# Expert layers of a decoder trunk in written program order, with a new start and a half-fp32 output projection

## The chip, the cores and the metric

The kernel runs on one core of a Trainium2 chip. The metric is the time of one execution in microseconds (us): the median over the runs shown. Five engines work side by side, each on its own queue of instructions: TensorE (PE in the profile, PEld for its weight loads), VectorE (DVE), ScalarE (ACT), GpSimd (POOL) and SyncE (SP), which here only starts DMA transfers. An engine waits on semaphores for the others; the program is scheduled ahead of time, so what stands in an engine's queue, and in which order, is fixed when it is built.

## The reference

Two layers over 256 tokens of width 1024. Layer 0 mixes tokens by a short gated convolution, layer 1 by differential attention; each is followed by a PEER expert layer. Every sub-layer is modulated by shift, scale and gate vectors made from `c`, and ended by a layer norm. Cut to what matters here:

```python
def ada_mod(c, w, b):
    m = jax.nn.silu(c) @ w + b
    shift, scale, gate = jnp.split(m, 3, axis=-1)
    return shift[:, None, :], 1.0 + scale[:, None, :], 1.0 + gate[:, None, :]

def short_conv_mixer(h, w_in, conv_w, w_out):
    gb, gc, xv = jnp.split(h @ w_in, 3, axis=-1)
    z = gc * xv
    zc = conv_w[0] * zp[:, 0:S] + conv_w[1] * zp[:, 1:S + 1] + conv_w[2] * zp[:, 2:S + 2]
    return (gb * zc) @ w_out

def peer_ffn(h, w_q, sub_keys, u, v):          # 8 heads, 2 x 128 keys, 16384 experts
    q = (xc @ w_q).reshape(PEER_CHUNK, PEER_HEADS, 2, PEER_HALF)
    s = jnp.einsum('thpd,pnd->thpn', q, sub_keys)
    sv, si = lax.top_k(s, PEER_TOPK)            # top 16 of each half
    cand_s = sv[:, :, 0, :, None] + sv[:, :, 1, None, :]
    top_s, pos = lax.top_k(cand_s, PEER_TOPK)   # top 16 of the pairs
    g = jax.nn.softmax(top_s, axis=-1)
    act = jax.nn.gelu(jnp.einsum('td,thkd->thk', xc, u[idx]), approximate=False)
    return jnp.einsum('thk,thkd->td', g * act, v[idx])

# per layer: h = x*scale + shift; f = mixer(h) or peer_ffn(h)
#            x = layer_norm(ALPHA * x + gate * f, ln_g, ln_b)
```

## The kernel before

The expert layer doesn't gather: it computes all 128 x 128 experts densely and masks. Experts come in 128 blocks of 128. A **w_q step** (16 of them) projects the queries, and a **U step** (128) the pre-activations of one block; each is 24 matmuls of 256 columns, because every fp32 operand is split into a high and a low fp32r part and three products are summed (`mm3`, lines 141 to 143). After two U steps ScalarE runs a gelu (L805) into `ring`. A **V step** (128) is 12 matmuls of 512 columns into the four accumulators `acc` (L874). A **G step** (`G_step`, 32 for each of three chunks of 46, 42 and 40 blocks) turns the picked expert numbers into a mask: DVE builds two one-hot tiles A and B (L825 to L829), PE multiplies them (L838) and DVE multiplies the result into `ring` (L840).

Each weight tile of 512 KB is loaded by SP into a `raw` buffer and split: ACT copies the high part (L87), DVE subtracts to get the low part (L90; shown as `spt<-raw,spt`). `pipeline` starts the load and split of a step three steps ahead of its matmuls. The split tiles come from the pool `sp` of ten buffers, the raw ones from six (`STREAM`).

The picks are made beside this. `halves` takes the top 16 of each half of the keys (five DVE operations for each of 16 heads-and-halves and two token tiles), two such pieces after every w_q step from the fifth on. `topk(t)` then handles the pairs: sums in `cand`, eight heads of five operations, a softmax (an exp on ACT, L735, between DVE operations), twelve small operations on `f`, two rounds of one-hot look-ups (`eq` on DVE, `keys` copied by ACT, L766 to L774), and three PE transposes. A piece stands after every U step of the first chunk.

`fill` computes modulation vectors of later sub-layers: one column of `ada_w` is a 512 KB load and one DVE operation over 128 x 1024 (L177, `raw<-raw,csb`). In the expert layers it runs in the gaps of the third and last V chunk. `late` applies the norm's gain and bias to X (L297) for the residual, `prep` makes the gain and bias rows for the next norm.

Before the expert layers stands layer 0's convolution. `csb`, the silu of `c` on all partitions, is a 512 KB broadcast load; X comes as one load of 1 MB (L207 transposes it). `project_out` (L352) multiplies the convolution's output `y` by its weights, again in three products. Norm sums are L266 and L268; L286 writes the normalised X.

What sets the order: `ordered` pins DMA starts to program order while the convolution layer is built; after it, the scheduler that builds the program places every instruction by its own estimate of when it can run. Inside the expert layers all engines follow that scheduler, not the text.

Of the kernel before, what the change touches and what calls it, by code (L numbers as in the profile page):

```python
# [37 lines left out]
SPBUFS = 10  # L38
STREAM = 6
# [4 lines left out]
def tile_trunk(ctx: ExitStack, tc: tile.TileContext, x, c, columns, ada_w, ln_g, ln_b, conv_w_in_a, conv_w_in_b,  # L44
# [3 lines left out]
    dve, act, pool, pe = nc.vector, nc.scalar, nc.gpsimd, nc.tensor  # L48
# [99 lines left out]
    nc.sync.dma_start(csb, rows_bcast(c[0], D))  # L148
    X = const.tile([P, NT, D], F32, name="X")

# [14 lines left out]
    act.activation(csb, csb, AF.Silu)  # L165
# [7 lines left out]
    def ada_column(i, s, part, n, dst):  # L173

        w = raw()
# [3 lines left out]
    def ada_unit(i, s, part):  # L179
        a = small.tile([P, KC], F32, tag="ada", name="ada", bufs=2)  # L180
        for q in range(KC // 2):
            for f in [ada_column(i, s, part, n, a[:, n:n + 1]) for n in (2 * q, 2 * q + 1)]:
                f()
            yield
        at = slice(None), 2 * i + s, slice(KC * part, KC * part + KC)
        dve.tensor_tensor(mod[at], a, ada_bT[at], op=ALU.add)
        yield
# [30 lines left out]
    def ln_params(i, s):  # L218
        gb = raw(), raw()
# [15 lines left out]
    class Norm:  # L235
# [56 lines left out]
        def affine(self, _):  # L292

            gb = ln_params(self.i, self.s)
            for t in range(NT):
                for n, op in enumerate((ALU.mult, ALU.add)):
                    dve.tensor_tensor(X[:, t, :], X[:, t, :], gb[n], op=op)  # L297

# [39 lines left out]
    def project_out(w, yT, accs, engs):  # L338
        def first(q):
            return [load(w[(2 * q + kk) * P:(2 * q + kk + 1) * P, :], engs[kk]) for kk in range(2)]  # L340

        def second(q, parts):
            if q == 0:
                accs.extend(new_accs())
            yh, yl = yT[q]
            for t in range(NT):
                rows = slice(t * P, (t + 1) * P)
                for kk, (wh, wl) in enumerate(parts):
                    k = 2 * q + kk
                    for lhs, rhs, first, last in ((yh, wh, True, False), (yh, wl, False, False), (yl, wh, False, True)):  # L350
# [7 lines left out]
    def conv_mixer(j, hT, cp, fill, prep):  # L358
        gbT = [None] * KC
        gcT = [None] * KC  # L360
        yh = cp.tile([P, KC, T], F32R, name="yh")
        yl = cp.tile([P, KC, T], F32R, name="yl")

        def use(n, ps):
# [9 lines left out]
            y = cp.tile([P, T], F32, tag="y", name="y", bufs=2)  # L374
# [4 lines left out]
            dve.tensor_tensor(y, y, gbT[k], op=ALU.mult)  # L379
            copy(yh[:, k, :], y)  # L380
            last["y"] = sub(dve, yl[:, k, :], y, yh[:, k, :].bitcast(F32))
# [7 lines left out]
        def h_first(q):  # L389
# [3 lines left out]
            if q == 0:  # L393
# [623 lines left out]
```

## Time and profile before

| | before |
|---|---|
| median of 3 runs | 1957.79 us (1957.78 to 1961.25) |
| profiled execution | 1956.54 us |
| its span, first to last instruction | 1954.8 us |
| PE busy | 1885.1 us, 96% of the span |
| DVE busy | 1550.6 us, 79% |
| ACT busy | 905.3 us, 46% |
| mean granted TensorE clock | 0.988 |
| HBM read | 375.42 MB, 193 GB/s over the span |

The profile is of one execution, 1.25 us below the median. The span leaves 1.7 us outside of it. "Busy" is the union of an engine's instructions; the span minus PE's busy time, 69.7 us, is all that PE stood still. Matmuls overlap in the trace (a record of 283 ns begins every 120 ns or so), so PE's pace is read from counts in a stretch, not from the length of one record.

### The profile page before, as it was taken

To read this page: it belongs to the slowest core of one execution; us is meant where nothing else is said; L and a number is where in the kernel's file an instruction comes from. 1 tells how busy PE (TensorE), PEld (TensorE's weight loads), DVE (VectorE), ACT (ScalarE), POOL (GpSimd) and SP (SyncE) were. 2 spreads that over 40 slices of the span, in tenths; PEclk is the share of its full clock that TensorE was granted. 3 is DMA by queue.
4 is the path that set the end of the run, shared out by engine and by line. 5 is a ranking of instruction groups with operands and counts; after the bars stand their busy time and mean duration, and the time that the engine had idled before them with its cause. 6 is when DMAs were issued, how large, how long until landed. Compare 5 with 4: busy or idle time off the path is not lost.

```text
span 1954.8 us, 36946 instructions
## 1 busy us (share of the span) xinstructions
PE 1885.1 (96%) x14858; PEld 1720.6 (88%) x14858; DVE 1550.6 (79%) x3138; ACT 905.3 (46%) x1191; POOL 9.5 (0%) x28
## 2 busy tenths in 40 slices
PE   7969999999999999989899899999999999999897
PEld 6969999999999988867798799999999999888786
DVE  7989887887888888876677788878878766888755
ACT  4534555334444444434466545653444444444443
POOL 0000000000000000000100000000000000000000
PEclk9989999999999999999999999999999999999999
DMA  9955655556778765568753246555567555555563
GB/s 383 366 187 159 185 180 177 163 158 210 249 243 256 232 201 173 173 198 279 241 182 111 86 152 184 183 174 161 161 208 226 173 175 181 168 169 181 173 194 97
DMA packets 104412, 378.87 MB, mean 194 GB/s; under 512 B 11568, under 2 KB 12208, under 8 KB 104240
## 3 DMA queue, kind: packets, MB, share of 16 engines
q1 hardware_dynamic: 104096, 376.42, 59.8%
q8 instruction: 116, 1.90, 0.4%
q14 instruction: 56, 0.46, 0.1%
q10 hardware_dynamic: 144, 0.09, 0.0%
HBM read 375.42 MB, written 1.05 MB: 193 GB/s over the span
## 4 chain that ended last, share of the span: by engine, by line
PE 91%; DVE 5%; DMA 2%; issue 1%; ACT 1%; SPq 0%; DVEq 0%; ACTq 0%
PE acc L874 34%; PE ps L141 15%; PE ps L142 15%; PE ps L143 15%; PE ps L838 4%; DVE raw L177 2%; PE acc L352 2%; PE acc L142 2%; PE acc L141 2%; PE acc L143 2%; DVE spt L90 1%; DMA raw<-in_ada_w 1%; DMA X<-in_x 1%; PE ps L517 0%; DMA gsub<-in_attn_subln_g 0%
## 5 line engine op out<-in xcount | busy, mean ns | idle before, releaser
L87 ACT ACTIVATE spt<-raw 128x1024 fp32r<-128x1024 f32 x608 | 641.1, 1058 | 745.3 <-PE ps L142 416.5
L90 DVE TENSOR_TENSOR spt<-raw,spt 128x1024 fp32r<-128x1024 f32 x608 | 741.0, 1222 | 171.3 <-ACT spt L87 166.5
L141 PE MATMUL ps<-hh,spt 128*128 128x256 f32 x2400 | 684.9, 286 | 2.9 <-DVE hh L214 2.4
L142 PE MATMUL ps<-hl,spt 128*128 128x256 f32 x2400 | 681.0, 284 | 0.6 <-DVE hl L90 0.6
L143 PE MATMUL ps<-hh,spt 128*128 128x256 f32 x2400 | 680.5, 284 | 0.0
L874 PE MATMUL acc<-spt,wh 128*128 128x512 f32 x2048 | 565.9, 396 | 4.4 <-ACT wh L87 4.4
L141 PEld LDWEIGHTS ps<-hh,spt 128*128 128x128 f32 x2400 | 460.6, 192 | 6.8 <-issue 3.0
L142 PEld LDWEIGHTS ps<-hl,spt 128*128 128x128 f32 x2400 | 461.4, 192 | 4.0 <-DVE hl L90 0.9
L143 PEld LDWEIGHTS ps<-hh,spt 128*128 128x128 f32 x2400 | 461.3, 192 | 0.0
L874 PEld LDWEIGHTS acc<-spt,wh 128*128 128x128 f32 x2048 | 375.9, 188 | 75.8 <-ACT wh L87 4.6
L874 PE MATMUL acc<-spt,wl 128*128 128x512 f32 x1024 | 319.6, 392 | 3.6 <-DVE wl L90 3.6
L874 PEld LDWEIGHTS acc<-spt,wl 128*128 128x128 f32 x1024 | 191.9, 188 | 44.8 <-DVE wl L90 5.1
L177 DVE SCALAR_TENSOR_TENSOR raw<-raw,csb 128x1024 f32<-128x1024 f32 x96 | 116.1, 1223 | 57.8 <-DMA raw<-in_ada_w 57.7
L87 ACT ACTIVATE wh<-ring 128x512 fp32r<-128x512 f32 x128 | 79.9, 627 | 159.0 <-PE acc L874 148.9
L840 DVE SCALAR_TENSOR_TENSOR ring<-ps,ring 128x368 f32<-128x368 f32 (+2 forms) x192 | 98.1, 512 | 68.6 <-PE ps L838 68.0
L825 DVE TENSOR_TENSOR A<-iota_e,jT 128x1024 f16<-128x1024 f16 x192 | 131.0, 683 | 0.0
L829 DVE TENSOR_TENSOR B<-B,gT 128x368 f16<-128x368 f16 (+2 forms) x384 | 125.1, 334 | 4.0
L90 DVE TENSOR_TENSOR wl<-ring,wh 128x512 fp32r<-128x512 f32 x128 | 88.0, 689 | 38.7 <-ACT wh L87 38.2
L838 PEld LDWEIGHTS <-A 128*128 128x128 f16 x3072 | 91.0, 96 | 31.1 <-issue 14.3
L838 PE MATMUL ps<-B,A 128*128 128x46 f16 (+2 forms) x3072 | 111.7, 182 | 6.6 <-DVE B L829 6.6
L805 ACT ACTIVATE ring<-ps 128x512 f32<-128x512 f32 x128 | 74.7, 584 | 33.8 <-PE ps L143 33.7
L827 DVE TENSOR_TENSOR B<-iota_e,iT 128x368 f16<-128x368 f16 (+2 forms) x192 | 63.4, 331 | 0.0
(204 smaller groups left out, 1179.9 us busy)
## 6 DMA issues: line engine op xcount, KB each, us to landing
raw<-in_peer_u SPq DMA_DIRECT2D x256, 512.0 KB, 3.8
raw<-in_peer_v SPq DMA_DIRECT2D x256, 512.0 KB, 3.9
raw<-in_ada_w SPq DMA_DIRECT2D x96, 512.0 KB, 4.7
raw<-in_peer_w_q SPq DMA_DIRECT2D x32, 512.0 KB, 4.1
raw<-in_attn_w_qk SPq DMA_DIRECT2D x16, 512.0 KB, 4.4
raw<-in_conv_w_in_a SPq DMA_DIRECT2D x12, 512.0 KB, 10.2
raw<-in_conv_w_in_b SPq DMA_DIRECT2D x12, 512.0 KB, 10.2
raw<-in_conv_w_out SPq DMA_DIRECT2D x8, 512.0 KB, 7.2
```

The lines of the kernel that those rows point to most:

```text
L87: act.activation(o, i, AF.Copy, scale=scale)
L90: return eng.tensor_tensor(o, a, b, op=ALU.subtract)
L141: pe.matmul(ps, ah, bh, start=first, stop=False)
L142: pe.matmul(ps, ah, bl, start=False, stop=False)
L143: pe.matmul(ps, al, bh, start=False, stop=last)
L177: return lambda: dve.scalar_tensor_tensor(w, w, 1.0, csb, op0=ALU.mult, op1=ALU.mult, accum_out=dst)
L805: act.activation(ring[:, s:s + 2, :].rearrange("p j t -> p (j t)"), st["ps"], AF.Gelu)
L825: dve.tensor_tensor(by_two(A), numbers(0, KEYS), pairs(jT, KEYS), op=ALU.is_equal)
L829: dve.tensor_tensor(by_two(B[:, h]), by_two(B[:, 1]), pairs(gT[:, h], n), op=ALU.mult)
L838: pe.matmul(ps[:, t, :], A[:, t, :], B[:, h, t, :], start=h == 0, stop=h == 1)
L840: dve.scalar_tensor_tensor(r, ps.rearrange("p t j -> p j t"), 1.0 / GSCALE, r, op0=ALU.mult, op1=ALU.mult)
L874: pe.matmul(acc[t][hf], lhs[:, jj, rows], rhs[:, hf * 512:(hf + 1) * 512], start=first and jp == 0 and jj == 0, stop=last and last_pair an ...
```

## The change

Four edits. First, in both expert layers every instruction of PE, DVE and ACT, and every load of SP, is kept in program order from the end of the w_q loop on (`pinned`, and the wrapper `InOrder`); the `yield None` that flushed the pipeline there is gone. Second, the room for this: `cand`, `f`, `eq` and `keys` of `topk` get fixed places in the ring's spare part instead of `sp` buffers, `SPBUFS` goes from 10 to 9 and `STREAM` from 6 to 5, and two `side` buffers carry the columns of `fill` and the rows of `late`, each column loaded one turn ahead of its use; `fill` runs two turns in three instead of a pair every second or third step, and `late` is cut into three pieces nearer the end of the layer. Third, the start: `c` is loaded as one 4 KB row and spread by two fp32 matmuls with a row of ones, and X is loaded in four quarters of 256 columns. Fourth, of the convolution's output projection rows 512 to 1023 are multiplied in plain fp32, unsplit: 16 matmuls of 512 columns with operand `yf` and raw weights in place of 48 split ones; four splits of weights and four of `y` go.

```diff
-SPBUFS = 10
-STREAM = 6
+SPBUFS = 9
+STREAM = 5
...
+    class InOrder:
...
+        def __getattr__(self, name):
+            def call(*a, **k):
+                ins = getattr(self.engine, name)(*a, **k)
+                if pinned:
+                    tc.keep_in_program_order(ins)
+                return ins
...
+    dve, act, pe = (InOrder(e) for e in (nc.vector, nc.scalar, nc.tensor))
...
-            if ordered:
+            if ordered or pinned:
                 tc.keep_in_program_order(ins)
...
-    nc.sync.dma_start(csb, rows_bcast(c[0], D))
+    crow = raw()[0:1, :]
+    act.dma_start(crow, c)
...
+    def load_x(q):
+
+        cols = slice(q * 256, (q + 1) * 256)
+        (sync if q else act).dma_start(X[:, :, cols], x[0][:, cols].rearrange("(t p) d -> p t d", p=P))
...
-    act.activation(csb, csb, AF.Silu)
+    for hf in range(2):
+        ps, cols = bank(), slice(hf * 512, (hf + 1) * 512)
+        pe.matmul(ps, ones, crow[:, cols], start=True, stop=True)
+        act.activation(csb[:, cols], ps, AF.Silu)
...
+    def ada_units(*which, tile=raw):
...
+            for n in range(KC):
+                f = ada_column(i, s, part, n, a[:, n:n + 1], tile)
+                if loaded:
+                    compute(*loaded)
+                    yield
+                loaded = at, a, f, n == KC - 1
...
+                    if q >= whole:
+                        products = (yT[q][0], ws[0], True, True),
+                    else:
+                        (yh, yl), (wh, wl) = yT[q], ws
+                        products = (yh, wh, True, False), (yh, wl, False, False), (yl, wh, False, True)
...
+        cand = scratch(PH * NCAND).rearrange("p (h k) -> p h k", **hk)
+        f = scratch(6 * P).rearrange("p (n k) -> p n k", n=6)
+        eq, keys = (scratch(1024).bitcast(F16).rearrange("p (h k a) -> p h k a", h=PH, k=TOPK) for _ in range(2))
...
-            yield None
+            pinned.append(True)
...
-                if n % 2 == 1:
+                if n % 3 != 0:
                     yield advance(fill)
...
-                if n == 6:
-                    yield None, late
+                if n == n2 - 10:
+                    yield drain(fill)
+                    yield advance(rest)
                 if n == n2 - 8:
-                    yield drain(fill)
                     yield None, prep
+                if n in (n2 - 7, n2 - 5):
+                    yield advance(rest)
 
         pipeline(steps(), 3)
+        pinned.clear()
```

In the changed kernel the wrapper records the instructions, so all of them stand at its line, L59, and names tell them apart. The first place is ACT in layer 0's first chunk of U steps, at the first `topk`. `ring<-ps 128x512` is a gelu, `ring<-ring 128x128` the exp of the softmax, `ring<-ring 128x2048` (before: `keys`) the copy of the keys, `spt<-raw` a weight split. Before:

```order
L805 ACTIVATE ring<-ps 128x512
L87 ACTIVATE spt<-raw 128x1024 x2
L735 ACT_TABLE_LOAD
L735 ACTIVATE ring<-ring 128x128
L87 ACTIVATE spt<-raw 128x1024
L805 ACT_TABLE_LOAD
L805 ACTIVATE ring<-ps 128x512
L87 ACTIVATE spt<-raw 128x1024 x2
L805 ACTIVATE ring<-ps 128x512
L87 ACTIVATE spt<-raw 128x1024
L805 ACTIVATE ring<-ps 128x512
L87 ACTIVATE spt<-raw 128x1024
L87 ACTIVATE keys<-ring 128x2048
```

Now:

```order
L59 ACTIVATE ring<-ps 128x512
L59 ACT_TABLE_LOAD
L59 ACTIVATE ring<-ring 128x128
L59 ACTIVATE spt<-raw 128x1024 x2
L59 ACT_TABLE_LOAD
L59 ACTIVATE ring<-ps 128x512
L59 ACTIVATE ring<-ring 128x2048
L59 ACTIVATE spt<-raw 128x1024 x2
L59 ACTIVATE ring<-ps 128x512
L59 ACTIVATE ring<-ring 128x2048
L59 ACTIVATE spt<-raw 128x1024 x2
L59 ACTIVATE ring<-ps 128x512
```

The exp and its table load stood ahead of a gelu with splits between; now each of exp and the key copies stands directly behind the gelu that closes a pair of U steps.

The second place is DVE at the end of layer 0's w_q loop. `ql<-ps,qh` makes the low part of a query that PE waits for, `MAX`, `MAX_INDEX` and `MATCH_REPLACE` are the pieces of `halves`. Before:

```order
L90 TENSOR_TENSOR spt<-raw,spt 128x1024
L693 MAX_INDEX ring<-ring 128x8
L90 TENSOR_TENSOR ql<-ps,qh 128x256
L693 MAX_INDEX ring<-ring 128x8 x4
L694 MATCH_REPLACE ring<-ring 128x128 x5
L90 TENSOR_TENSOR spt<-raw,spt 128x1024
L694 MATCH_REPLACE ring<-ring 128x128
L90 TENSOR_TENSOR ql<-ps,qh 128x256
L694 MATCH_REPLACE ring<-ring 128x128 x2
L695 MAX ring<-ring 128x8 x6
L90 TENSOR_TENSOR spt<-raw,spt 128x1024
```

Now:

```order
L59 TENSOR_TENSOR ql<-ps,qh 128x256
L59 MAX ring<-ring 128x8
L59 MAX_INDEX ring<-ring 128x8
L59 MATCH_REPLACE ring<-ring 128x128
L59 MAX ring<-ring 128x8
L59 MAX_INDEX ring<-ring 128x8
L59 MAX ring<-ring 128x8
L59 MAX_INDEX ring<-ring 128x8
L59 MATCH_REPLACE ring<-ring 128x128
L59 MAX ring<-ring 128x8
L59 MAX_INDEX ring<-ring 128x8
L59 TENSOR_TENSOR spt<-raw,spt 128x1024
```

Between two `ql` there stood one operation over eight halves, or part of one; now ten dependent operations on two halves stand there, and PE's `kh,ql` products follow in the same step instead of a step later.

The third place is DVE where layer 0's last G steps give way to the third V chunk. `B<-B,gT` are parts of a G step's tiles, `ring<-ps,ring` its end, `raw,ada<-raw,csb` a column of `fill`, `wl<-ring,wh` the low part of a V step's left operand, `X<-X,raw` is `late`. Before:

```order
L829 TENSOR_TENSOR B<-B,gT 128x320 x2
L177 SCALAR_TENSOR_TENSOR raw,ada<-raw,csb 128x1024
L829 TENSOR_TENSOR B<-B,gT 128x320
L177 SCALAR_TENSOR_TENSOR raw,ada<-raw,csb 128x1024
L840 SCALAR_TENSOR_TENSOR ring<-ps,ring 128x40x8 x2
L90 TENSOR_TENSOR wl<-ring,wh 128x512 x2
L297 TENSOR_TENSOR X<-X,raw 128x1024 x2
L90 TENSOR_TENSOR spt<-raw,spt 128x1024
L297 TENSOR_TENSOR X<-X,raw 128x1024 x2
L90 TENSOR_TENSOR wl<-ring,wh 128x512
L90 TENSOR_TENSOR spt<-raw,spt 128x1024 x2
L90 TENSOR_TENSOR wl<-ring,wh 128x512
```

Now:

```order
L59 SCALAR_TENSOR_TENSOR ring<-ps,ring 128x40x8
L59 TENSOR_TENSOR A<-iota_e,jT 128x1024
L59 TENSOR_TENSOR B<-iota_e,iT 128x320
L59 TENSOR_TENSOR B<-B,gT 128x320 x2
L59 TENSOR_TENSOR spt<-raw,spt 128x1024
L59 SCALAR_TENSOR_TENSOR ring<-ps,ring 128x40x8
L59 TENSOR_TENSOR wl<-ring,wh 128x512
L59 TENSOR_TENSOR spt<-raw,spt 128x1024
L59 SCALAR_TENSOR_TENSOR ring<-ps,ring 128x40x8
L59 TENSOR_TENSOR spt<-raw,spt 128x1024
L59 TENSOR_TENSOR wl<-ring,wh 128x512
L59 TENSOR_TENSOR spt<-raw,spt 128x1024 x2
```

Columns of `fill` stood between the tiles of the last G steps, and `late` came right behind them; now no such operation stands there, and the first column follows five rows below.

## Rows read from the trace of the kernel before

**Rows 1.** The page: busy time of each engine, share and instructions.

```profile
PE 1885.1 (96%) x14858; PEld 1720.6 (88%) x14858; DVE 1550.6 (79%) x3138; ACT 905.3 (46%) x1191; POOL 9.5 (0%) x28
```

**Rows 2.** Windows: stretch, length, busy PE PEld DVE ACT POOL, PEclk, DMA share, GB/s.

```profile
100.00:125.00 25.00, 14.06 (x61) 11.08 (x59) 24.38 (x45) 4.38 (x7) 0.00 (x0) 0.88 0.65 211
...
225.00:250.00 25.00, 25.00 (x210) 25.00 (x210) 17.66 (x51) 13.61 (x15) 0.00 (x0) 1.00 0.63 195
...
848.00:860.00 12.00, 4.78 (x46) 3.90 (x46) 9.67 (x20) 3.40 (x5) 0.00 (x0) 0.84 0.79 250
...
1825.00:1836.50 11.50, 6.60 (x85) 4.89 (x84) 9.07 (x18) 4.35 (x6) 0.00 (x0) 1.00 0.40 133
```

**Rows 3.** Waits from 836 to 972 us: sum in us, times, longest.

```profile
DVE raw L177 <- DMA raw<-in_ada_w: 21.8, 11, 3.5
...
PE ps L838 <- DVE B L829: 4.2, 2, 3.0
...
PE acc L874 <- DVE wl L90: 2.4, 2, 1.3
```

**Rows 4.** Waits of PE in the first 60 us.

```profile
PE ps L207 <- DMA X<-in_x: 9.4, 1, 9.4
```

**Rows 5.** Timeline of ACT and DVE at the start: start, length, instruction, idle before.

```profile
5.53 1.06 ACT L165 ACTIVATE csb<-csb 128x1024 f32<-128x1024 f32 x1 [3.09 <-DMA csb<-in_c]
...
6.96 1.23 DVE L177 SCALAR_TENSOR_TENSOR raw<-raw,csb 128x1024 f32<-128x1024 f32 x1 [1.07 <-DMA raw<-in_ada_w]
...
16.45 1.23 DVE L90 TENSOR_TENSOR spt<-raw,spt 128x1024 fp32r<-128x1024 f32 x1 [4.31 <-ACT spt L87]
```

**Rows 6.** Timeline of DVE around the convolution's norm.

```profile
104.00 1.22 DVE L177 SCALAR_TENSOR_TENSOR raw<-raw,csb 128x1024 f32<-128x1024 f32 x1
...
114.31 1.22 DVE L177 SCALAR_TENSOR_TENSOR raw<-raw,csb 128x1024 f32<-128x1024 f32 x1
...
115.45 1.29 DVE L266 TENSOR_TENSOR spt<-acc,rows 128x512 f32<-128x512 f32 x2
...
127.85 0.81 DVE L286 TENSOR_SCALAR X<-spt,mv 128x1024 f32<-128x1024 f32 x1
```

**Rows 7.** Timeline of PE in the attention, where fp32 operands are not split.

```profile
1012.96 0.60 PE L551 MATMUL ps<-v,aT 128*128 128x128 f32 x4
...
1013.52 0.28 PE L141 MATMUL acc<-hh,spt 128*128 128x256 f32 x1
```

**Rows 8.** The chain that ended last: start us, us, what, with its count.

```profile
91.76 9.30 PE acc L352 x40
...
1836.57 107.32 PE acc L874 x472
```

**Rows 9.** Groups of instructions by form, 150 to 330 us: count | busy, mean ns.

```profile
L805 ACT ACTIVATE ring<-ps 128x512 f32<-128x512 f32 x23 | 13.6, 591 | 16.9 <-PE ps L143 16.9
L693 DVE FIND_INDEX8 ring<-ring 128x8 uint32<-128x128 f32 x32 | 8.6, 285 | 0.0
...
L87 ACT ACTIVATE keys<-ring 128x2048 f16<-128x2048 f16 x4 | 7.6, 1906 | 8.2 <-PE ps L142 8.2
...
L90 DVE TENSOR_TENSOR ql<-ps,qh 128x256 fp32r<-128x256 f32 x12 | 5.0, 415 | 0.0
L770 DVE TENSOR_TENSOR eq<-eq,keys 128x2048 f16<-128x2048 f16 x4 | 4.9, 1226 | 5.3 <-ACT keys L87 5.3
L766 DVE TENSOR_TENSOR eq<-ring,iota_a 128x2048 f16<-128x2048 f16 x4 | 4.9, 1219 | 0.0
...
L773 DVE TENSOR_TENSOR eq<-eq 128x1024 f16<-128x1024 f16 x4 | 2.8, 689 | 0.1
...
L751 DVE SCALAR_TENSOR_TENSOR f<-f 128x128 f32<-128x128 f32 x2 | 0.6, 293 | 0.1
```

**Rows 10.** Timeline of ACT at the first exp.

```profile
229.69 1.28 ACT L735 ACT_TABLE_LOAD   x1
230.99 0.31 ACT L735 ACTIVATE ring<-ring 128x128 f32<-128x128 f32 x1
```

More of the change, by code (lines that the diff above doesn't have):

```diff
@@ L171, in tile_trunk, with side, ada_column, compute @@
     mod = const.tile([P, 4, 24], F32, name="mod")
-    def ada_column(i, s, part, n, dst):
-        w = raw()
+    def side():
+        return stream.tile([P, D], F32, tag="side", name="side", bufs=2)
+    def ada_column(i, s, part, n, dst, tile=raw):
+        w = tile()
         sync.dma_start(w, ada_w[i, s, part, n])
         return lambda: dve.scalar_tensor_tensor(w, w, 1.0, csb, op0=ALU.mult, op1=ALU.mult, accum_out=dst)
[L179 to L186, printed above, removed]
+    def ada_units(*which, tile=raw):
+        def compute(at, a, f, final):
+            f()
+            if final:
+                dve.tensor_tensor(mod[at], a, ada_bT[at], op=ALU.add)
+        loaded = None
+        for i, s, part in which:
+            a = small.tile([P, KC], F32, tag="ada", name="ada", bufs=3)
+            at = slice(None), 2 * i + s, slice(KC * part, KC * part + KC)
+            for n in range(KC):
[4 more added lines that the diff above has]
+                loaded = at, a, f, n == KC - 1
+        compute(*loaded)
         yield
@@ L297, in affine @@
                     dve.tensor_tensor(X[:, t, :], X[:, t, :], gb[n], op=op)
+                yield
     def abank():
@@ L336, in drain, with project_out @@
         return None, second
-    def project_out(w, yT, accs, engs):
+    def project_out(w, yT, accs, engs, whole=KC):
         def first(q):
-            return [load(w[(2 * q + kk) * P:(2 * q + kk + 1) * P, :], engs[kk]) for kk in range(2)]
+            parts = []
+            for kk in range(2):
+                rows = w[(2 * q + kk) * P:(2 * q + kk + 1) * P, :]
+                if q >= whole:
+                    parts.append((raw(),))
+                    sync.dma_start(parts[-1][0], rows)
+                else:
+                    parts.append(load(rows, engs[kk]))
+            return parts
         def second(q, parts):
@@ L344, in second @@
                 accs.extend(new_accs())
-            yh, yl = yT[q]
             for t in range(NT):
                 rows = slice(t * P, (t + 1) * P)
-                for kk, (wh, wl) in enumerate(parts):
+                for kk, ws in enumerate(parts):
                     k = 2 * q + kk
-                    for lhs, rhs, first, last in ((yh, wh, True, False), (yh, wl, False, False), (yl, wh, False, True)):
+                    if q >= whole:
+                        products = (yT[q][0], ws[0], True, True),
+                    else:
+                        (yh, yl), (wh, wl) = yT[q], ws
+                        products = (yh, wh, True, False), (yh, wl, False, False), (yl, wh, False, True)
+                    for lhs, rhs, first, last in products:
                         for hf in range(2):
@@ L373, in use @@
             dve.tensor_tensor(z[:, 2:], ps, gcT[k], op=ALU.mult)
-            y = cp.tile([P, T], F32, tag="y", name="y", bufs=2)
+            half = KC // 2
+            y = yf[:, k - half, :] if k >= half else cp.tile([P, T], F32, tag="y", name="y", bufs=2)
             col = lambda w: smT[:, 160 + 8 * w + k:161 + 8 * w + k]
@@ L629, in steps @@
                 if h0 == 4:
-                    yield None, late
+                    yield drain(late())
             yield None, prep
@@ L926, in steps @@
                 yield v
+            rest = late(side)
             for n, v in enumerate(vs(2)):
                 yield v
-                if n % 3 == 2:
+                if n % 3 != 0 and n < n2 - 10:
                     yield advance(fill)
-                if n == 6:
-                    yield None, late
+                if n == n2 - 10:
+                    yield drain(fill)
+                    yield advance(rest)
                 if n == n2 - 8:
-                    yield drain(fill)
                     yield None, prep
+                if n in (n2 - 7, n2 - 5):
+                    yield advance(rest)
         pipeline(steps(), 3)
+        pinned.clear()
         return acc
-    def units(*which):
-        for w in which:
-            yield from ada_unit(*w)
     with tc.tile_pool(name="cp", bufs=1) as cp, tc.tile_pool(name="cs", bufs=12) as more:
@@ L953, in tile_trunk @@
     ordered.clear()
-    fill = units((0, 1, 2), (1, 0, 0), (1, 0, 1), (1, 0, 2), (1, 1, 0), (1, 1, 1))
+    fill = ada_units((0, 1, 2), (1, 0, 0), (1, 0, 1), (1, 0, 2), (1, 1, 0), (1, 1, 1), tile=side)
     with tc.tile_pool(name="pp", bufs=1) as pp:
@@ L966, in tile_trunk @@
         late, norm = norm.affine, Norm(1, 1, None, ada)
-        acc = peer(1, hT, pp, units((1, 1, 2)), norm.prepare, late)
+        acc = peer(1, hT, pp, ada_units((1, 1, 2), tile=side), norm.prepare, late)
     norm(acc)
```

48 lines of the change are left out of this document (28 added, 20 removed).

## The prediction

> **What bounds the kernel now.** The page comes first: PE is busy for 1885.1 us, 96% of the span, so at most 69.7 us can come from PE's waiting [rows 1]. Where those lie is read from windows. In the stretches of plain U and V steps PE has no idle time at all: 25.00 of 25.00 us with 210 matmuls, which makes a U step of 24 matmuls 24/210 x 25 = 2.86 us [rows 2]. The idle time lies in a few places: the start, where PE waits 9.4 us for X [rows 4]; the norm after the convolution, where PE is busy for 14.06 of 25 us while DVE is busy for 24.38 [rows 2]; the last G steps of layer 0, with 4.78 busy of 12.00 us [rows 2]; and the same place in layer 1, 6.60 of 11.50 us [rows 2]. The waits of layer 0's G tail say why: DVE stood 21.8 us, in 11 pieces, for columns of `ada_w`, and PE waited for DVE's B tiles and low parts [rows 3]. So the kernel is PE's work plus some places where PE waits for DVE, and each edit is worth what it removes or adds there.
>
> **G tails (a gain).** With the order of the change no column of `fill` and no piece of `late` stands among the last G tiles, and columns come from buffers of their own, loaded a turn ahead. Gone are the idle 12.00 - 4.78 = 7.2 us of layer 0 and 11.50 - 6.60 = 4.9 us of layer 1 [rows 2], and 2.4 us of waits for `wl` [rows 3]. In the 12-us stretch the granted clock is 0.84 [rows 2]. Between the levels 1.2 and 2.4 GHz that is 32%, 3.8 us, at the lower one, which costs up to 1.9 us. Sum: 7.2 + 1.9 + 2.4 + 4.9 = 16.4 us. Below: 12, if only the two large ones go. Above: 19, if the idle time just beyond these windows goes as well.
>
> **Start and convolution's end (a gain).** DVE's first column starts at 6.96 us, after ACT waited 3.09 us for the broadcast of `c`; it then stands 4.31 us for a split queued on ACT behind the transposed X [rows 5]. With a 4 KB row and X in quarters the first column starts some 0.7 us earlier, and the 4.31 us are filled; but two splits, 1.15 us each, now stand ahead of the first modulation. 0.7 + 4.3 - 2.3 = 2.7 us, with bounds 0 and 5. The unsplit half costs PE time. From 1012.96 to 1013.52 us there are four fp32 records of 128 columns and one split matmul of 0.12 us: 0.44 / 4 = 0.11 us for a record, and the program issues two for one product [rows 7]. A product of 512 columns is then 4 x 0.22 = 0.88 us, 16 make 14.1 us. The 48 split ones take 9.30 / 40 = 0.23 us each [rows 8], 11.2 us: PE loses 2.9 us. (Were an unsplit product no dearer than a split one, it would gain 11.2 - 3.7 = 7.5 us; the nearest row is fp32 itself, so I take the loss.) What it buys lies on DVE. Before, ten columns stand back to back from 104.00 to 115.45 us, 1.15 us apart, ahead of the norm's first sum, with four more inside the norm, and the last X is ready at 127.85 + 0.81 = 128.66 us [rows 6]. After, four weight and four `y` subtractions are gone and columns run two a step, so DVE's queue is through when PE is. PE ended its products at about 114.06 [rows 2]; now 114.1 - 2.7 + 2.9 = 114.3; then the sums of the second token tile (1.3 and 1.2), one or two columns or splits between (1.2 to 2.4), small operations (0.5) and the two X writes (1.6): 120 to 121.3 us. Both together: 128.7 - 121 = about 7 us, bounds 3 and 10.
>
> **End of the w_q loop (a loss).** Program order puts ten top-k operations between two `ql`, and PE needs `ql` in the same step. DVE's round is a split of 1.15 us, `ql` at 0.4, and ten operations of 285 ns or a little less with short value loads between [rows 9]; back to back they would be 2.5 us, end to end 3.3; I take 3.0. Sum 4.5 us, against PE's 2.86 + 0.6 = 3.45. The steps 12 to 15 run so in the new order; with some lead at first that makes 0.75 + 0.95 + 1.05 + 1.05 = 3.8 us a layer, 7.6 in all, bounds 3 (lead from earlier steps lasts) and 10.
>
> **Top-k in program order (a loss).** Before, PE had no wait here: the transposes stood where their operands were ready. Now each ACT piece stands behind the gelu of an odd U step, which waits for that step's matmuls. Count from the start of the step behind which the softmax stands. Matmuls 2.86, then the gelu 0.6 and 0.2 between: 3.6 us [rows 9]; a table load of 1.28 and the exp of 0.31 [rows 10]: 5.3. From there DVE has, in order, the rest of the softmax 0.8, five splits at 1.15, twelve small operations at up to 0.29 with overlap 3.2, two comparisons of 1.22, two products of 1.23, and twice the adds, 0.69 and three shorter ones, 1.8 [rows 9]: 0.8 + 5.75 + 3.2 + 4.9 + 3.6 = 18.25. The key copies, 1.91 us each behind the next two gelus [rows 9], end at 11.3 and 17.0, before DVE wants them. So DVE has the transposes' operands at 23.55 us; PE comes to them after seven steps, at 20.0. It waits 3.55 us, and as the queue is in order nothing else can run: two token tiles in two layers, 14.2 us. Bounds: 0, if DVE enters with a lead of over a step; 20, if splits run late too. What is queued behind the waiting transposes is only the next U step, which has its operands.
>
> **At no cost.** One `sp` buffer less leaves a split three steps of lead, 8.6 us against 1.15 + 1.06 of work. The moved `late` and the loads of `side` are covered by the 40 V steps of the third chunk, 2.7 us each (472 matmuls in 107.32 us, twelve a step [rows 8]), in which DVE has 1.15 + 0.35 of split work and at most one column of 1.22. Were that cover gone, a column would cost its wait, 2 us in the mean [rows 3].
>
> **Sum.** 1956.54 - 16.4 - 7 + 7.6 + 14.2 = 1954.9 us for a profiled execution like the one shown; the median lies 1.25 us above it, so 1956 us.
>
> **Rivals.** (1) *DVE has its lead, and top-k waits hardly come* (faster). Against it: DVE's operations lie one behind the other in this count, with 18.25 us of work from 5.3 on. For it: DVE is busy for only 17.66 of 25 us where the top-k began before [rows 2]. It gives 1956 - 14 = 1942, and 1934 if the w_q waits fail too. (2) *Start and norm give more, or the w_q loop loses less*: 1950 us. (3) *A lower clock behind each top-k wait* (slower). After PE's wait of 3.0 us in layer 0's G tail the stretch shows 0.84 [rows 2, 3]; the new waits are as long. Four times 1.9 us is 7.6: 1964 us. It decides from waits of about 3 us on. The Trainium skill, page "TensorE: Matmul & The Clock Gate", section "What's actually happening", says that the throttled state is the default and activity releases it; by that rule, too, the new waits could cost twice, and the rows here agree. (4) *Columns of `side` arrive late and DVE, in order, holds splits behind them*: ten such waits of 2 us of which half reach PE add 10 us, 1966; it decides when a load takes longer than its turn. (5) *A drain at each table switch*. The row shows the exp 20 ns after the load's end (229.69 + 1.28 against 230.99) [rows 10]. The Trainium skill, page "ScalarE: Activation LUTs", section "What ACT_TABLE_LOAD costs", counts a drain of 1.38 us on top of the load. Did it stand on this chain, each top-k wait would grow by 1.4 us, four by 5.6: 1962 us; the row speaks against it.
>
> **How the numbers follow.** Forecast 0.35 (own range 1951 to 1962); rival 1 0.27; rival 2 0.10; rival 3 0.18; rival 4 0.08; rival 5 0.02. Within 0.2% (3.9 us, about what a measurement of this kernel can tell from no change) lie the forecast and half of rival 5: 0.36. Faster: rivals 1 and 2, 0.37. Slower: 0.27. The range takes in 1942 and 1966 with some room and leaves out rival 1's lower half and the far end of rival 4: 1938 to 1968.
>
> **What would show it.** In the profile after: PE's wait for X at the start gone, the norm's wait about 6 us; no idle PE ahead of the third V chunk; four waits of PE for a DVE operation on `ring` of about 3.5 us each in the two first U chunks; PE short by some 1 us a step in the last four w_q steps. The prediction is wrong if the first U chunks show 25 of 25 us for PE, if the G tails still have idle time, or if DVE waits for `side` in the third V chunk.

## The result and the profile after

The changed kernel takes 2037.41 us (median of 4 runs, 2037.11 to 2038.47) against 1957.78 us for the kernel before: a ratio of 1.0403, 95% interval 1.0385 to 1.0421. It is slower by 80 us, where no change was forecast. The profiled execution took 2038.47 us, its span is 2036.7 us, 81.9 us longer than before.

The page of the changed kernel begins so (busy time of each engine), and its chain that ended last (the work that led to the end, followed back from the last instruction) has this share by engine:

```profile
PE 1930.9 (95%) x14846; PEld 1730.8 (85%) x14846; DVE 1588.5 (78%) x3130; ACT 878.1 (43%) x1184; POOL 13.9 (1%) x29
...
PE 80%; DVE 10%; ACT 3%; DMA 3%; issue 3%; SPq 0%; ACTq 0%; DVEq 0%
```

Before, the chain was

```profile
PE 91%; DVE 5%; DMA 2%; issue 1%; ACT 1%; SPq 0%; DVEq 0%; ACTq 0%
```

PE has 12 matmuls less than before [rows 1] and yet 46 us more of busy time, so long waits are not the whole story: short ones vanish under overlapping records, and slower matmuls count as busy. Where the time went is read by cutting both traces at PE's own marks: the last transpose of the normalised X ahead of the w_q loop (its first matmul follows some 2 us later), the first G matmul, the last U matmul and the last V matmul of each layer (us; the last column is the fastest version found, told below).

| stage | before | after | difference | e11 |
|---|---|---|---|---|
| start to last transpose ahead of w_q | 130.8 | 126.2 | -4.6 | 127.3 |
| w_q and first U chunk, layer 0 / 1 | 196.2 / 197.2 | 214.3 / 211.5 | +18.1 / +14.3 | 201.7 / 202.6 |
| G with U, then V with U, layer 0 / 1 | 374.0 / 374.0 | 375.3 / 375.3 | +1.3 / +1.3 | 377.7 / 373.9 |
| last U to last V, layer 0 / 1 | 271.4 / 263.5 | 303.3 / 275.8 | +31.9 / +12.3 | 257.8 / 257.8 |
| attention and the norms around it | 136.5 | 144.3 | +7.8 | 137.5 |
| end | 11.3 | 10.7 | -0.6 | 10.7 |

More than half is in the stage that was forecast to gain. Four windows of the changed kernel, columns as in [rows 2]: the convolution's norm, the first top-k, the middle of the last V chunk of layer 0 and its end.

```profile
100.00:125.00 25.00, 19.24 (x58) 10.59 (x57) 21.08 (x44) 6.31 (x10) 0.00 (x0) 0.91 0.69 231
250.00:275.00 25.00, 21.87 (x171) 21.64 (x170) 22.97 (x47) 14.22 (x16) 0.00 (x0) 0.93 0.47 151
...
900.00:925.00 25.00, 22.18 (x87) 16.62 (x85) 14.84 (x21) 7.80 (x9) 0.00 (x0) 0.93 0.70 261
975.00:1000.00 25.00, 14.27 (x62) 10.17 (x60) 11.36 (x19) 8.01 (x10) 0.00 (x0) 0.89 0.66 236
```

The norm is better than before (19.24 us of PE against 14.06 in [rows 2]). The first U chunk has lost 3.1 us and some of the granted clock; before, the same window was full:

```profile
250.00:275.00 25.00, 25.00 (x211) 25.00 (x210) 23.88 (x72) 15.87 (x20) 0.00 (x0) 1.00 0.56 169
```

In the V chunk no engine is full: PE is busy for 14.27, DVE for 11.36 of 25 us. Who waits there? First SP, then ACT, from 865 to 1019 us:

```profile
SPq L88 <- DVE side L59: 88.7, 19, 11.9
...
ACT spt L59 <- DMA raw<-in_peer_v: 70.2, 25, 10.5
```

And in the G steps before it, PE from 716 to 865 us:

```profile
PE ps L59 <- DVE B L59: 9.3, 20, 0.8
```

### The profile page after: what moved, and what is told of

Same layout as the page of the kernel before. It is cut to its first block, busy times and chain, and to the rows that moved or that the text cites. A ratio compares the mean times of both kernels' runs of the same rounds, so it can differ in the third digit from the quotient of the medians.

```text
span 2036.7 us, 36861 instructions
## 1 busy us (share of the span) xinstructions
PE 1930.9 (95%) x14846; PEld 1730.8 (85%) x14846; DVE 1588.5 (78%) x3130; ACT 878.1 (43%) x1184; POOL 13.9 (1%) x29
## 4 chain that ended last, share of the span: by engine, by line
PE 80%; DVE 10%; ACT 3%; DMA 3%; issue 3%; SPq 0%; ACTq 0%; DVEq 0%
PE ps L59 46%; PE acc L59 35%; DVE spt L59 4%; DMA raw<-in_peer_v 3%; DVE ring L59 3%; ACT spt L59 2%; DVE B L59 1%; DVE A L59 1%; ACT ring L59 1%; DVE side L59 1%; DMA smT<-in_columns 0%; ACT s L59 0%; DVE raw L59 0%; SPq L88 0%; DVE ql L59 0%
## 5 line engine op out<-in xcount | busy, mean ns | idle before, releaser
L59 DVE TENSOR_TENSOR spt<-raw,spt 128x1024 fp32r<-128x1024 f32 x604 | 731.9, 1220 | 272.5 <-ACT spt L59 230.6
L59 PE MATMUL ps<-hh,spt 128*128 128x256 f32 x4864 | 920.1, 286 | 2.6 <-DVE hh L59 2.4
L59 PEld LDWEIGHTS ps<-hh,spt 128*128 128x128 f32 x4864 | 777.5, 193 | 7.1 <-issue 1.9
L59 ACT ACTIVATE spt<-raw 128x1024 fp32r<-128x1024 f32 x604 | 617.7, 1051 | 218.6 <-DMA raw<-in_peer_v 90.9
L59 PE MATMUL ps<-hl,spt 128*128 128x256 f32 x2432 | 693.2, 285 | 0.0
L59 PE MATMUL acc<-spt,wh 128*128 128x512 f32 x2048 | 578.6, 402 | 18.9 <-ACT spt L59 14.6
L59 PEld LDWEIGHTS ps<-hl,spt 128*128 128x128 f32 x2432 | 470.5, 194 | 3.7 <-DVE hl L59 0.3
L59 PEld LDWEIGHTS acc<-spt,wh 128*128 128x128 f32 x2048 | 374.1, 189 | 105.0 <-ACT spt L59 18.5
L59 PE MATMUL acc<-spt,wl 128*128 128x512 f32 x1024 | 323.6, 395 | 0.0
L59 ACT ACTIVATE ring<-ps 128x512 f32<-128x512 f32 x128 | 76.5, 597 | 456.6 <-PE ps L59 456.3
L59 PEld LDWEIGHTS acc<-spt,wl 128*128 128x128 f32 x1024 | 193.1, 189 | 45.7
L59 ACT ACTIVATE wh<-ring 128x512 fp32r<-128x512 f32 x128 | 80.1, 626 | 276.5 <-PE acc L59 266.6
L59 DVE TENSOR_TENSOR wl<-ring,wh 128x512 fp32r<-128x512 f32 x128 | 88.1, 689 | 86.6 <-ACT wh L59 86.6
L59 DVE TENSOR_TENSOR B<-B,gT 128x368 f16<-128x368 f16 (+2 forms) x384 | 129.0, 336 | 13.2
L59 DVE TENSOR_TENSOR A<-iota_e,jT 128x1024 f16<-128x1024 f16 x192 | 130.8, 681 | 0.0
L59 PEld LDWEIGHTS <-A 128*128 128x128 f16 x3072 | 90.9, 96 | 46.6 <-DVE B L59 24.0
L59 PE MATMUL ps<-B,A 128*128 128x46 f16 (+2 forms) x3072 | 112.8, 182 | 18.5 <-DVE B L59 18.5
L59 DVE SCALAR_TENSOR_TENSOR ring<-ps,ring 128x368 f32<-128x368 f32 (+2 forms) x192 | 97.0, 505 | 0.0
L59 PE MATMUL acc<-hh,spt 128*128 128x256 f32 x384 | 74.2, 292 | 10.1 <-ACT hh L59 9.5
L59 PEld LDWEIGHTS acc<-hh,spt 128*128 128x128 f32 x384 | 62.9, 199 | 11.5 <-ACT hh L59 9.9
L59 DVE SCALAR_TENSOR_TENSOR side<-side,csb 128x1024 f32<-128x1024 f32 x56 | 68.1, 1217 | 0.0
L59 DVE TENSOR_TENSOR B<-iota_e,iT 128x368 f16<-128x368 f16 (+2 forms) x192 | 63.0, 328 | 0.0
```

Source lines behind the costliest of these rows:

```text
L59: ins = getattr(self.engine, name)(*a, **k)
```

## The experiments

Runs e1 to e4 each change one thing in the changed kernel. The first theory was that all of the loss is waits in the in-order queues, named by stage; the rivals were the smaller number of buffers, bandwidth, and the matmul pitch (the distance from the start of one matmul to the start of the next). Runs e5 to e7 are built one on another, e10 on e6, e11 on e10, e12 and e13 on e11; e8 and e9 start from the kernel before.

**e1, place of the operands.** In the last V chunk of layer 1, where nothing waits, V steps take 2.8 us instead of 2.7. Only addresses differ there: the `ones` row came first in its pool and moved `wh` and `wl` by 2944 bytes.

```diff
-ones = wk.tile([1, P], F32, tag="B", name="ones")
+ones = wk.tile([1, P], F32, tag="wh", name="ones")
```

> The change as it is, with the row of ones put into the first-named pair of buffers of its pool, so that wh and wl lie again where they lay in the kernel before (from 113440 and 121632 instead of 116384 and 124576 bytes); the order of the instructions is the same on every engine. Theory P (place): in the V steps of the changed kernel matmuls of 512 columns begin every 229 to 238 ns, in the kernel before every 227, with no wait between, because the stationary operand now lies elsewhere in memory than the moving one. Then the V steps go back to 227 ns and about 21 us come back: 2016 us. Rival (order or traffic): the pitch comes from what the other engines and loads do meanwhile; then it stays at 229 to 238 and the time at 2037 us.

Measured: 2029.91 us (2026.54 to 2033.08). Matmuls of that stage in 25 us (1925 to 1950), changed kernel first, then e1:

```profile
L59 PE MATMUL acc<-spt,wh 128*128 128x512 f32 x72 | 19.9, 395 | 0.0
L59 PE MATMUL acc<-spt,wl 128*128 128x512 f32 x36 | 11.3, 395 | 0.0
```

```profile
L59 PE MATMUL acc<-spt,wh 128*128 128x512 f32 x76 | 20.3, 389 | 0.0
L59 PE MATMUL acc<-spt,wl 128*128 128x512 f32 x36 | 11.1, 389 | 0.0
```

There are 112 instead of 108 in the same time, none after a wait, and nearly every start-to-start distance is 226 or 227 ns again, with the same order of instructions. Theory P holds, at a third of its price: 7.5 us of 21. Layer 1's last V chunk falls from 126.7 to 123.2 us; where PE waits for DVE or for loads anyway (layer 0's last chunk, 154.1 us before the edit and 156.5 with it) a faster matmul wins nothing.

**e2, no program order.** `pinned.append(True)` is again `yield None`; everything else stays.

> The change without keeping program order in the expert layers (the flush of the pipeline stands there again); buffers, fill, start and convolution as in the change. Theory O (order): the waits in the w_q loop, at the transposes of top-k, in the third U chunk's G steps and in layer 0's last V chunk are all those of in-order queues; without them some 65 to 75 us go: 1962 to 1972 us, with the slower matmul pitch left. Rival (buffers): nine split buffers, five raw ones and the two side buffers cause the waits; then most stay and the time is over 2005 us.

Measured: 2021.62 us (2015.79 to 2023.27). Neither theory: from the last U to the last V step it takes 270.6 and 268.9 us, so those waits are gone, but in layer 0 PE stands for 32 us at the first transpose of top-k (PE's waits from 129 to 365 us):

```profile
PE ps L59 <- DVE ring L59: 32.1, 1, 32.1
```

The transpose stands behind as many U matmuls as in both other kernels; its operand comes late. The scheduler has put columns of `fill` between the operations of top-k on DVE, 23 of them from 200 to 297 us, where the kernel before has none:

```profile
L59 DVE SCALAR_TENSOR_TENSOR side<-side,csb 128x1024 f32<-128x1024 f32 x23 | 28.5, 1246 | 0.8 <-DMA side<-in_ada_w 0.8
```

The time lies where the rival put it, but not for its reason. So the order is not worth 70 us against this scheduler: taken away alone it makes room for a worse order. Undoing one part of a change that was made as a whole answers what that part is worth there, not what it costs.

**e3, side loads on a queue of their own.** POOL issues the columns of `fill` instead of SP.

```diff
-        sync.dma_start(w, ada_w[i, s, part, n])
+        if tile is side:
+            tc.keep_in_program_order(pool.dma_start(w, ada_w[i, s, part, n]))
+        else:
+            sync.dma_start(w, ada_w[i, s, part, n])
```

> The change with the loads of the side columns issued by POOL instead of SP, everything else the same. Theory S: in layer 0's last V chunk SP stands 88.7 us, 19 times, at a side load whose buffer DVE has not freed yet, and the V loads queued behind it come late; DVE frees the buffer only behind splits that wait for those V loads. On a queue of their own the side loads hold up nothing, and the stage from the last G step to the last V step falls from 154 us to about 130: 2013 us. Rival (bandwidth): the V loads are late because memory is busy; then the stage keeps its 154 us and the time 2037 us.

Measured: 2020.5 us (2020.12 to 2023.24). The stage from the last G to the last V step falls from 154.1 to 136.2 us. Waits of ACT for V loads in it, which had been 25 with 70.2 us in all:

```profile
ACT spt L59 <- DMA raw<-in_peer_v: 11.3, 2, 11.0
```

Theory S holds, bandwidth doesn't; one wait of 11 us is left where SP stands 15.9 us, once, at a load of `late`, which still goes from SP into a `side` buffer.

**e4, columns earlier.** One column after every step of the third U chunk, one after every third in the last V chunk.

```diff
-                if n % 3 != 0:
-                    yield advance(fill)
+                yield advance(fill)
...
-                if n % 3 != 0 and n < n2 - 10:
+                if n % 3 == 2 and n < n2 - 10:
```

> The change with a fill column after every step of the third U chunk (40 columns instead of 26) and after one in three of the last V chunk's steps (as few as remain). Theory S: fewer side loads in the last V chunk, fewer blocked V loads: about half of the 24 us lost there comes back, and the third U chunk has DVE time for 14 more columns or loses a few us: 2025 to 2030 us. Rival (bandwidth): no change, 2037 us; rival (DVE is full in the third U chunk): 2045 us or more.

Measured: 2012.27 us (2009.69 to 2014.44), 25 us faster and more than expected. The stage takes 126.9 us, as long as layer 1's 126.7. This run moves DVE's columns as well as their loads; e3 moved only the loads and took 18 of the 27 us, with one blocked load left. Together they put the 27 us down to the blocked queue. In the trace of the changed kernel the chain is seen in SP's and ACT's timelines of the same stretch (start, length, instruction):

```profile
898.35 0.33 SPq L88 DMA_DIRECT2D side<-in_ada_w  x1
898.77 0.86 SPq L88 DMA_DIRECT2D raw<-in_peer_v  x2
901.23 0.33 SPq L88 DMA_DIRECT2D side<-in_ada_w  x1
901.65 0.38 SPq L88 DMA_DIRECT2D raw<-in_peer_v  x1
908.39 0.33 SPq L88 DMA_DIRECT2D side<-in_ada_w  x1
```

```profile
897.35 1.06 ACT L59 ACTIVATE spt<-raw 128x1024 fp32r<-128x1024 f32 x1 [0.91 <-DMA raw<-in_peer_v]
903.17 1.06 ACT L59 ACTIVATE spt<-raw 128x1024 fp32r<-128x1024 f32 x1 [4.76 <-DMA raw<-in_peer_v]
```

A side load waits for the buffer that DVE frees by the column two back. DVE reaches that column only behind splits that need V loads, and those stand behind the side load on SP: from 902.0 to 908.4 us nothing is issued. In e4 SP still stands at side loads (865 to 992 us), but ACT waits for no V load any more, so these six waits stay within the lead of the loads:

```profile
SPq L88 <- DVE side L59: 35.2, 6, 6.3
```

Runs e5 to e7 are built on e1 and e4 together.

**e5, `wh` one step later.** In the changed kernel the DVE queue around a G step reads so:

```profile
735.13 0.69 DVE L59 TENSOR_TENSOR wl<-ring,wh 128x512 fp32r<-128x512 f32 x1 [0.78 <-ACT wh L59]
736.08 1.23 DVE L59 TENSOR_TENSOR spt<-raw,spt 128x1024 fp32r<-128x1024 f32 x1 [0.26 <-ACT spt L59]
737.22 0.49 DVE L59 SCALAR_TENSOR_TENSOR ring<-ps,ring 128x320 f32<-128x320 f32 x1
737.62 0.68 DVE L59 TENSOR_TENSOR A<-iota_e,jT 128x1024 f16<-128x1024 f16 x1
738.22 0.32 DVE L59 TENSOR_TENSOR B<-iota_e,iT 128x320 f16<-128x320 f16 x1
738.58 0.69 DVE L59 TENSOR_TENSOR B<-B,gT 128x320 f16<-128x320 f16 x2
```

`wl` waits for ACT's `wh`, which waits for PE to free the buffer of the pair two back; the G tiles behind it are ready at 739.27, and PE had wanted them at 738.2.

```diff
                     s = (2 * jp) % RING
                     w = ring[:, s:s + 2, :]
+                    st["ring"] = w
+                if jj == 1:
+                    w = st["ring"]
                     st["w"] = [wk.tile([P, 2, T], F32R, tag=n, name=n) for n in ("wh", "wl")]
```

> The change with wh and wl in their old place, with the fill columns in the third U chunk as in the run before (these two together should stand at about 2003 us by their single effects), and with the copies wh and wl of a pair of V steps made one step later. Theory W: in the change ACT's wh waits for the pair two back, DVE's wl behind it, and the G tiles queued behind wl come about 1 us late, 20 times a layer; one step later the buffer is free and the waits go. The stage from the last U to the last G step falls from 147.5 to about 136 us in both layers: 1980 us. Rival: DVE has too much work in that stretch and the waits move elsewhere: 2000 us or more.

Measured: 1981.21 us (1976.28 to 1982.42). The stage from the last U to the last G step takes 134.5 us in both layers, from 147.5 in e1, and PE has no wait in it (window 720 to 857 us):

```profile
720.00:857.00 137.00, 137.00 (x1064) 109.90 (x1063) 128.32 (x231) 57.36 (x68) 0.00 (x0) 1.00 0.58 183
```

Theory W holds: 13 us a layer where 11.5 were expected, with DVE still busy for 128 of 137 us. DVE was not short of time, it stood in the wrong order. A part is lost again in layer 0: its third U chunk with V steps, now with 40 columns in it, takes 247.1 us against 240.0 in layer 1.

**e6, transposes later.** Two empty steps ahead of the first token tile's transposes, one ahead of the second's.

```diff
+            yield
+            if t == 0:
+                yield
             ps = bank()
             pe.transpose(ps[:, 0:P], f[:, 4, :], ident)
...
-                yield drain(aux) if n == n0 - 5 else advance(aux, 1, ())
+                yield drain(aux) if n == n0 - 4 else advance(aux, 1, ())
```

> The run before it in this list with the three transposes of top-k two U steps later for the first token tile and two for the second. Theory T: each of PE's four waits of 3.3 us at the transposes goes, and with it the stretch at half clock behind it (0.93 mean clock over 25 us, about 1.7 us each): 19 to 20 us less than that run. Rival: DVE is late as a whole and the wait comes back at the next split: under 8 us less.

Measured: 1967.47 us (1962.24 to 1969.3), 13.7 us less by medians; the profiled spans differ by 19.2 us. In the changed kernel PE's waits from 160 to 325 us are these; in e6 from 200 to 330 us the row below them is all that PE waits:

```profile
PE ps L59 <- DVE ring L59: 6.3, 2, 3.1
PE acc L59 <- DVE ql L59: 2.0, 3, 1.3
PE acc L59 <- ACT qh L59: 1.4, 3, 0.5
```

```profile
PE ps L59 <- DVE ring L59: 0.3, 1, 0.3
```

The stage from the last transpose ahead of w_q to the first G matmul is 205.2 and 201.4 us, 7.2 and 10.5 less than in e5: 17.7 of the 19 to 20 us expected; attention is some 4 us longer. Theory T holds.

**e7, flush ahead of the pinned part** (`yield None` put back ahead of `pinned.append(True)`).

> The run before it in this list with the pipeline flushed ahead of the pinned part, so that the last w_q steps are scheduled as in the kernel before and only what follows is kept in order. Theory Q: the 7 to 8 us a layer that the end of the w_q loop loses come from ql standing behind ten top-k operations; half to all of 15 us goes. Rival: the pieces of top-k only move into the U steps, where DVE has no room, and nothing is won: within 4 us.

Measured: 1961.06 us (1956.4 to 1964.45). The stage is 206.0 and 202.7 us, not shorter than in e6. What this run has less lies in attention, 144.5 against 149.6 us, which the edit doesn't touch; the profiled spans differ by 1.5 us. Not confirmed. Counted by matmuls, PE loses its time about two steps later than in e6, and no less of it. In this run the flush also has a price of its own: from 185 to 195 us the loads stand still, and behind that PE has the lower clock (DMA share 0.00, then PEclk 0.50, which is 1.2 GHz):

```profile
185.00:190.00 5.00, 3.67 (x31) 3.38 (x29) 5.00 (x35) 0.38 (x1) 0.00 (x0) 1.00 0.00 0
190.00:195.00 5.00, 1.90 (x8) 1.46 (x9) 3.05 (x8) 4.20 (x6) 0.00 (x0) 0.81 0.00 0
195.00:200.00 5.00, 5.00 (x25) 5.00 (x25) 4.86 (x12) 2.89 (x3) 0.00 (x0) 0.50 0.87 274
```

**e8, start and convolution alone**, put into the kernel before (with `ones` placed as in e1).

> The kernel before with the two edits of the start and the convolution alone (c by TensorE, X by quarters, half of the output projection in fp32), expert layers and buffers as before. Theory: 4 to 7 us are won ahead of the first expert layer, where the changed kernel reaches its w_q loop 4.6 us earlier, and nothing changes behind it: 1952 to 1955 us. Rival: the scheduler places the rest otherwise, and the time is anywhere within 10 us of before.

Measured: 1954.94 us (1951.59 to 1956.86), ratio 0.9984, interval 0.9974 to 0.9993. The last transpose ahead of w_q starts at 127.3 instead of 130.8 us, and no stage behind it changes by more than 0.6 us: 3.5 us.

**e9, fewer buffers alone.** e8 with `SPBUFS = 9` and `STREAM = 5`.

> The kernel before with the start and convolution edits (1954.9 us) and only the numbers of buffers changed: nine split and five raw ones, no program order, no side buffers. Theory B: the 8 to 13 us that the attention stage loses in the changed kernel and in every variant of it, kept in order or not, come from the one split buffer and the one raw buffer less; attention goes from 136.7 to about 145 us, and the scheduler's U steps lose some as well: 1965 to 1985 us. Rival: attention loses by the way late, fill and the stages before it are ordered; then this run stays within 3 us of 1955.

Measured: 1967.03 us (1963.41 to 1971.71), 12 us more than e8. Attention with its norms takes 151.4 us instead of 136.7: theory B holds for the two pools together; which of them it is was not tried. Part of it is a wait of PE that e8 does not have there, while the changed kernel has it at the same length:

```profile
PE ps L572 <- DVE s L570: 5.7, 1, 5.7
```

The w_q loop and first U chunk lose nothing (196.8 and 195.8 us), the G steps behind it 1.3 us a layer.

**e10, two at once.** `halves` handles both token tiles, `topk` two heads, operation by operation; the core of it:

```diff
+                for sv, si, sl in both:
+                    dve.max(sv[:, 0:8], sl)
+                for sv, si, sl in both:
+                    dve.max_index(si[:, 0:8], sv[:, 0:8], sl)
+                for sv, si, sl in both:
+                    dve.match_replace(sl, sv[:, 0:8], sl, LOWEST)
+                yield
```

> The run with the later transposes (1967.5 us) with top-k's operations for both token tiles, and for two heads, alternating, so that an operation seldom follows the one whose result it reads; as many operations as before. Theory D: in the w_q loop DVE's round of 4.5 us holds some 0.8 us of waiting between dependent operations; w_q steps get shorter by 0.5 to 0.8 us where DVE is late and the stage from the start of the w_q loop to the first G step falls from 205 and 201 us to 197 to 200: 1958 to 1963 us. Rival: dependent operations cost nothing extra, or the loss sits elsewhere: within 2 us of that run.

Measured: 1959.46 us (1955.06 to 1962.28). The stage falls by 4.1 us in layer 0, to 201.1, and not in layer 1 (201.7). Half a confirmation: the rest of the 8 us lies in attention, which the edit does not touch (145.3 against 149.6 us).

**e11, ten split and four raw buffers** in the expert layers (`SPBUFS = 10`, `STREAM = 4`), six instead of four more raw ones in attention.

> The run before it in this list with ten split buffers, four raw ones in the expert layers and ten raw ones in the attention, as the kernel before has there. Theory B: the attention's 8 to 13 us come back, and a split may run a step earlier in the w_q loop: 1945 to 1953 us. Rival: four raw buffers are too few for loads of 4 us ahead of splits, and V or U steps wait for loads: over 1965 us.

Measured: 1950.89 us (1947.29 to 1958.13), ratio 0.9961, interval 0.9947 to 0.9975: 0.4% faster than the kernel before. Attention is back at 137.5 us, and loads with four buffers come in time. From the last U to the last V step PE has no idle time (two windows):

```profile
841.30:964.50 123.20, 123.20 (x553) 102.05 (x548) 80.53 (x94) 55.76 (x68) 7.09 (x9) 1.00 0.70 232
706.70:841.30 134.60, 134.60 (x1048) 107.64 (x1046) 125.86 (x227) 57.02 (x68) 0.00 (x0) 1.00 0.56 180
```

**e12, a shift of 32 bytes.** e11 with one tile of 32 bytes ahead of `wh`.

```diff
+wk.tile([P, 8], F32, tag="pad", name="pad", bufs=1)
 ones = wk.tile([1, P], F32, tag="wh", name="ones")
```

> The fastest version so far (1950.9 us: ten split and four raw buffers, all in-order waits mended) with wh, wl, A, B and what lies behind them shifted by 32 bytes; the order of the instructions is the same. Theory P32: what counts is where the stationary operand lies relative to the moving one within a small unit of memory; 32 bytes are enough, V matmuls go from 227 to 229 to 238 ns, the stage of 45 V steps from 123.2 to 126 us and the time to 1958 to 1962 us. Rival: only a larger offset counts; 123.2 us stay and the time with them, 1949 to 1953 us.

Measured: 1966.09 us (1964.45 to 1966.4), 15 us more than e11. The last V chunk of layer 1, with 554 matmul records in each, e12 first and e11 second:

```profile
1825.90:1952.60 126.70, 126.70 (x554) 102.16 (x550) 71.24 (x73) 55.26 (x67) 0.00 (x0) 1.00 0.54 178
```

```profile
1813.00:1936.20 123.20, 123.20 (x554) 102.10 (x550) 71.30 (x73) 55.22 (x67) 0.00 (x0) 1.00 0.56 183
```

Theory P32 holds: 231 to 235 ns between starts instead of 226 to 227, and at a higher price than the 7 to 11 us expected.

**e13, fill spread over two chunks**: one step in four of the second U chunk, three in four of the third.

> The fastest version so far with the columns of fill spread: one step in four of the second U chunk, three in four of the third, the rest in the last V chunk as now. Theory F: with 40 columns in it DVE is full in the third U chunk (243.7 us in layer 0 against 240.0 in layer 1, which has eight columns); with 30 it takes 240 to 241 us and the second chunk stays at 134: 1947 to 1949 us. Rival: the second chunk has no room either and gets longer by as much: 1950 to 1953 us.

Measured: 1952.78 us (1948.13 to 1954.87), no gain over e11. The third chunk stays at 243.5 us in layer 0, the second at 134.0, so the number of columns on DVE is not the cause. What may be, the waits of e11 in that stage show (SP, then PE, 464 to 706 us):

```profile
SPq L88 <- DVE side L59: 158.6, 37, 7.4
...
PE acc L59 <- DVE wl L59: 2.8, 3, 1.1
```

That would be the blocked queue of e4 again, in small: 37 waits of SP, and three of PE. Which of the 37 reach PE is not shown; a run that moves these loads to another queue in e11 was not made.

## Why the prediction was wrong, point by point

The forecast was 1956 us with a range to 1968; 2037 lies far outside. By its own steps:

- **At no cost** is the step that failed first. It covered the moved `fill` loads by time, 2.7 us a V step against one column of 1.22, and never asked what their issue does on SP's queue, in order too. They took 27 us of layer 0's last V chunk (e4). Rival 4 had the place and the direction, at 10 us and a chance of 0.08: it thought of slow loads that hold up DVE's queue, where the loads were not slow but not issued: SP stood 88.7 us for `side`, DVE did not.
- **G tails** failed as well. The old stalls did go, 12 us and more. But the step took it that nothing holds the tiles up once no column and no `late` stands among them. `wl` stands there, it waits for ACT, and ACT for a buffer that PE frees: 13 us a layer (e5). These two together with the pitch make the stage from the last U to the last V step +44.2 us where -16.4 was forecast, 60 of the 81 us.
- **One `sp` buffer less** was costed at nothing from the expert layers alone, and the raw buffer less was not costed. Attention uses both pools: 8 us here, 14.7 in e9.
- **Top-k in program order** was right in mechanism, place and size: four waits, two in each layer, of 3.1 us by the profile where 3.55 was worked out, and rival 3 came with them: the window from 250 to 275 us has a granted clock of 0.93 where the same steps had 1.00. The Trainium skill, page "TensorE: Matmul & The Clock Gate", section "What's actually happening", has the throttled state as the default that activity releases; this trace agrees. Waits and clock together are 7 to 10 us a layer, by e6 and its stage. The forecast and rival 3 were not rivals but one case.
- **End of the w_q loop**: forecast 3.8 us a layer. Counted by matmuls, the changed kernel loses 6.6 and 5.7 us there against before; the whole stage, after e6, is 9.0 and 4.2 us over. The place is right and the size too small. PE waits for `ql`, as forecast, but only 2.0 us, and 1.4 us for ACT's `qh`; two windows at the loop's end also have a lower clock, where before has 1.00. That the order of `ql` is all of the cause is not shown: neither e7 nor e10 took the loss away.

```profile
175.00:180.00 5.00, 3.69 (x24) 3.22 (x24) 5.00 (x27) 2.30 (x4) 0.00 (x0) 0.86 0.33 105
180.00:185.00 5.00, 4.51 (x29) 4.16 (x28) 4.15 (x20) 1.33 (x2) 0.00 (x0) 0.80 0.15 41
```

- **Start and convolution's end**: forecast 7, measured 4.6, in e8 3.5 us, inside its bounds. PE's wait for X is gone, but one for ACT's `hh` has come instead, 9.5 us, and that of the norm is the forecast 6 us.
- **The matmul pitch** was in no term: 7.5 us in e1, 15 in e12, where nothing else hides it.

The parts found, in us: blocked SP queue 27, `wl` 26, top-k 18, the w_q loop 13, the pitch some 10, fewer buffers 8, less 19 for the old G tails and 4.6 at the start. These make some 78 of the 81.9 of the spans; the sizes of w_q and pitch are the loosest.

## What to carry to other kernels

When code is put into program order, every wait in it becomes a wait for all that follows on that queue, the DMA queue first: follow each instruction that waits for a buffer to be freed, ask what stands behind it, and whether what frees the buffer is itself behind that. Issue such an instruction when its buffer is free, not as early as the code allows (e5 won 13 us in each layer), or so seldom that the lead of what stands behind it covers the wait (e4 won 25 us by medians). Cost a shared pool in every stage that uses it, and after an edit of the layout compare the start-to-start distance of plain matmuls before looking for waits.

## What the runs showed of the hardware

Where the two operands of a matmul lie in SBUF, the on-chip memory that holds these tiles, sets its pace. With `wh` and `wl` at the offsets of the kernel before, matmuls of 512 fp32r columns start every 226 or 227 ns; shifted by 2944 bytes most start every 229 to 238 (the changed kernel, put right in e1), shifted by 32 bytes every 231 to 235 (e12), with the same order of instructions and the clock at 1.00 in both windows. In e9 `wh` and `wl` lie 8192 bytes lower and the distance is 226 or 227 ns as well. In the good places `wh`, `wl` and the split tiles have the same offset to a multiple of 512 bytes; in the two bad ones they have not. That this is the condition is a guess from these layouts. The Trainium skill, page "SBUF — State Buffer", section "Operand start alignment", asks for multiples of the element size and says that this is about legality, not speed; both layouts keep that rule, and no run here says more about why.
